# Attention's products with V: two rounded products a key tile replaced by one float32 product, issued in two bursts a head

## The chip, the cores and the metric

The kernel runs on one core of one Trainium2 chip. The metric is the device time of one execution in microseconds; of several executions the median stands. A core has a matrix engine (TensorE, PE in the profile; its weight loads are listed apart as PEld), VectorE (DVE), ScalarE (ACT), GpSimd (POOL) and SyncE (SP), which issues most of the DMAs here. The engines run beside one another and wait for one another through semaphores. Each works off its own queue in order.

## What is computed

One inference step of a hybrid diffusion transformer with two layers: 1024 latent tokens (and 128 cached context tokens that they also read) and 128 tokens of a new prompt, model width 1024. Each layer mixes tokens in three ways side by side, grouped-query attention (GQA: 6 query heads, 2 key/value heads, width 64), latent attention (MLA: 4 heads) and a state-space model, projects the three together, and goes through an MLP. The change touches this part only:

```python
def block_attention(q, k, v, scale):
    ...
        s = jnp.einsum('bqgrd,bsgd->bgrqs', qblk, k).astype(F32) * scale
        pr = jax.nn.softmax(s, axis=-1).astype(v.dtype)
        return jnp.einsum('bgrqs,bsgd->bqgrd', pr, v)
```

All of it is in float32. Latent queries attend to 9 tiles of 128 keys (one of cached context, eight latent); queries of the new prompt attend to one tile, their own.

## The kernel before

**Precision.** Most products are made in the fast rounded type `fp32r`: a float32 operand is split into a rounded part and the rest (`cp`, line 65, casts; `lo`, line 78, subtracts), and the products of the parts are added up in PSUM. `mm` (line 69) issues a product, `tr` (line 73) a transpose against the identity. The modulation (`m<-raw,cT` in the profile) instead multiplies plain float32 tiles: four products of 32 columns of the array each, on quarters of it, side by side.

**Tiling of attention.** `mix` prepares keys and values, builds a list of 30 heads (a `Group` each) and calls `attn`. Queries come in three blocks `b` of 384 columns: blocks 0 and 1 hold latent queries, block 2 has 256 latent queries and 128 of the prompt. So there are 12 MLA heads ("first kind": three products a score tile, with `KT` and `KR`) and then 18 GQA heads ("second kind": two products, with `KY`) a layer. Of the 60 heads of both layers 40 have 384 columns and nine key tiles, 20 have 256 columns for the nine latent key tiles and 128 columns for key tile 9.

**One step.** The loop of `attn` goes over the heads and, in a head, over its key tiles `j`. A step j transposes the probabilities `P` of key tile j+2 into `pt` (PSUM; `trans`, two steps ahead), makes one score tile of the next head (`score`: products into `S`, and VectorE's copy with a running maximum, line 777, into `P`; after three of them ScalarE's exponential), and adds key tile j to the output `oT` (`prod`). `trans` splits the transposed tile: `ph` is ScalarE's cast and `pl` VectorE's subtraction. `prod` makes two products, with `ph` and with `pl`; the weights are `V(j)`, the rounded and the low part of the values side by side, 128 columns. So rows 0 to 63 of `oT` hold the sum with the rounded values and rows 64 to 127 that with the low parts. At the end of a head `fin1` copies `oT`, and `fin2` transposes it back, adds its two halves and scales by the row sums.

**Values.** The MLA values are made in the preamble of `mix` (ten tiles, each a ScalarE cast and a VectorE subtraction into `V`, line 919). The GQA values and keys are loaded in the background by `kv_gqa`, in four steps; the values are split by ScalarE and GpSimd into `VY`.

**Order of the work.** The program is written in the order of the loop, and a scheduler orders every engine's queue by priority, as a simulation of the timeline sees operands become ready. Between steps, `pull` lets background work (a state-space part, the output projection and post-norm of the block before, the modulation) issue a share that a small cost account (`spend`) allows. PSUM has two tiles `S`, three `pt`, one `oT`.

Of the kernel before, what the change touches and what calls it, by code (L numbers as in the profile page):

```python
# [4 lines left out]
F32 = mybir.dt.float32  # L5
R = mybir.dt.float32r
# [10 lines left out]
BK = 384  # L17
# [20 lines left out]
class Net:  # L38
# [711 lines left out]
    def attn(self, groups, tp, ps):  # L750
# [41 lines left out]
        def trans(g, j):  # L792
            rw = rows(g, j)
            c0, c1 = rw[0] * 128, rw[-1] * 128 + 128
            pt = ps.tile([128, BK], F32, name="pt", bufs=3)
            kc = j if j < 9 else 0
            for i in rw:
                self.tr(pt[:, i * 128:i * 128 + 128], g.P[i][:, kc * 128:kc * 128 + 128])
            ph = tp.tile([128, BK], R, name="ph", bufs=3)
            pl = tp.tile([128, BK], R, name="pl", bufs=3)  # L800
            self.cp(ph[:, c0:c1], pt[:, c0:c1])
            self.lo(pl[:, c0:c1], pt[:, c0:c1], ph[:, c0:c1])
            return ph[:, c0:c1], pl[:, c0:c1], c0, c1

        def prod(g, j, t):
            ph, pl, c0, c1 = t
            if j == 0:
                g.oT = ps.tile([128, BK], F32, name="oT", bufs=1)
            first, last = j in (0, 9), j in (8, 9)
            self.mm(g.oT[:, c0:c1], g.V(j), ph, first, False)  # L810
            self.mm(g.oT[:, c0:c1], g.V(j), pl, False, last)

# [23 lines left out]
        for n, g in enumerate(groups):  # L836
            nx = groups[n + 1] if n + 1 < ng else None
            nj = 9 if g.nq == 3 else 10
            ts = [trans(g, 0), trans(g, 1)]
            for j in range(nj):  # L840
                if j + 2 < nj:
                    ts.append(trans(g, j + 2))
                if nx and j < 9:
                    score(nx, j // 3, j % 3)
                prod(g, j, ts[j])
                if j == 1 and prev:
                    fin2(prev)
                if j == 5 and n + 2 < ng:
                    begin(groups[n + 2])
                self.pull(g.pull)  # L850
            fin1(g)
            prev = g
            if g.after:
                g.after()
# [13 lines left out]
    def mix(self, l):  # L868
# [50 lines left out]
        V = xm.tile([128, 10, 4, 2, 64], R, name="V")  # L919
        for j in range(10):  # L920
# [6 lines left out]
            self.cp(V[:, j, :, 0, :], p3)  # L927
            self.lo(V[:, j, :, 1, :], p3, V[:, j, :, 0, :])
# [20 lines left out]
        VY = kv.tile([128, 10, 2, 2, 64], R, name="VY")  # L949
        KY = kv.tile([128, 2, 1280], R, name="KY")  # L950
        self.bg += [self.kv_gqa(l, VY, KY, ss, blk), self.ssm_b(l, ss)]
# [13 lines left out]
        for b in range(NB):  # L965
            for h in range(4):
# [22 lines left out]
                groups.append(Group(b, prep, lambda j, h=h: V[:, j, h].rearrange("p v d -> p (v d)"),  # L989
# [10 lines left out]
        for b in range(NB):  # L1000
            for h in range(6):
# [33 lines left out]
                groups.append(Group(b, prep, lambda j, h=h: VY[:, j, h // 3].rearrange("p v d -> p (v d)"),  # L1035
# [275 lines left out]
    def kv_gqa(self, l, V, KT, tp, blk):  # L1311
        nc, a = self.nc, self.a
        for j0, j1 in ((0, 3), (3, 6), (6, 9), (9, 10)):
            n = j1 - j0
            kt = tp.tile([128, 3, 128], F32, name="zsl", bufs=2)
            vt = tp.tile([128, 3, 128], F32, name="zsl", bufs=2)
            for z, cache, scr in ((kt, "c_k", self.s_qk[:, :, 384:512]), (vt, "c_v", self.s_v)):
                f = 1 if j0 == 0 else 0
                if f:
                    self.dma(z[:, 0], a[cache][l].rearrange("p g d -> p (g d)"))  # L1320
                self.dma(z[:, f:n], scr[j0 + f - 1:j1 - 1].rearrange("t p c -> p t c"))
            yield D[4]
            v4 = vt[:, :n].rearrange("p t (g d) -> p t g d", d=64)
            for g in range(2):
                self.cp(V[:, j0:j1, g, 0, :], v4[:, :, g])
                self.lo(V[:, j0:j1, g, 1, :], v4[:, :, g], V[:, j0:j1, g, 0, :], nc.gpsimd)
# [296 lines left out]
```

## Time and profile before

| | before |
|---|---|
| median of 3 runs (lowest, highest) | 3482.16 us (3480.79, 3486.63) |
| the profiled execution | 3485.52 us |
| its span, first to last instruction | 3483.7 us |
| TensorE busy, share of the span | 3234.2 us, 93% |
| weight loads | 3055.2 us, 88% |
| VectorE | 2257.0 us, 65% |
| ScalarE | 1557.5 us, 45% |
| GpSimd | 1348.8 us, 39% |
| mean granted TensorE clock | 0.963 of full speed |

The table is the first part of the profile page. Busy shares are means over stages with different limits, so they say which engine has most to do, not which one sets the end of a given stage. A product's row gives the time from its start to the end of its drain; products overlap, so the time from one start to the next is shorter than the row's duration. Attention runs from 398 to 886 us in layer 0 and from 2130 to 2592 us in layer 1.

### The profile page before, as it was taken

To read this page: it belongs to the slowest core of one execution; us is meant where nothing else is said; L and a number is where in the kernel's file an instruction comes from. 1 tells how busy PE (TensorE), PEld (TensorE's weight loads), DVE (VectorE), ACT (ScalarE), POOL (GpSimd) and SP (SyncE) were. 2 spreads that over 40 slices of the span, in tenths; PEclk is the share of its full clock that TensorE was granted. 3 is DMA by queue.
4 is the path that set the end of the run, shared out by engine and by line. 5 is a ranking of instruction groups with operands and counts; after the bars stand their busy time and mean duration, and the time that the engine had idled before them with its cause. 6 is when DMAs were issued, how large, how long until landed. Compare 5 with 4: busy or idle time off the path is not lost. (4 is left out here: it accounts for less than half of the span.)

```text
span 3483.7 us, 50649 instructions
## 1 busy us (share of the span) xinstructions
PE 3234.2 (93%) x18578; PEld 3055.2 (88%) x18578; DVE 2257.0 (65%) x5318; ACT 1557.5 (45%) x3250; POOL 1348.8 (39%) x996
## 2 busy tenths in 40 slices
PE   6988799998899999999989887999888999999997
PEld 3966698788799999999989676989887999999997
DVE  6876888765647778774588767887658223333236
ACT  4464677665441221112454646787654411222223
POOL 6357432144651122113573673331356412111145
PEclk8989899999999999999999998999998999999999
DMA  5253333413332333322432533322233211111134
GB/s 212 80 175 104 115 86 116 164 49 97 126 103 80 94 99 98 91 91 73 145 120 97 170 112 111 89 92 67 79 108 98 85 37 45 41 43 43 37 97 145
DMA packets 164525, 340.71 MB, mean 98 GB/s; under 512 B 14429, under 2 KB 105909, under 8 KB 160693
## 3 DMA queue, kind: packets, MB, share of 16 engines
q1 hardware_dynamic: 161012, 335.32, 30.2%
q8 instruction: 146, 2.39, 0.3%
q10 hardware_dynamic: 3264, 2.16, 0.2%
q14 instruction: 103, 0.84, 0.1%
HBM read 280.99 MB, written 56.44 MB: 97 GB/s over the span
## 5 line engine op out<-in xcount | busy, mean ns | idle before, releaser
L78 POOL TENSOR_TENSOR w<-raw,w 128x1024 fp32r<-128x1024 f32 (+1 forms) x266 | 650.6, 2451 | 1370.8 <-ACT w L65 1314.8
L69 PE MATMUL g<-h,w 128*128 128x384 f32 x5328 | 971.5, 342 | 10.5 <-DVE h L78 6.4
L69 PEld LDWEIGHTS g<-h,w 128*128 128x128 f32 x5328 | 949.5, 190 | 16.5 <-DVE h L78 8.6
L69 PE MATMUL g<-big,w 128*128 128x384 f32 x4608 | 818.7, 336 | 8.4 <-DVE big L78 3.4
L69 PEld LDWEIGHTS g<-big,w 128*128 128x128 f32 x4608 | 802.5, 189 | 12.4 <-DVE big L78 5.2
L65 ACT CAST w<-raw 128x1024 fp32r<-128x1024 f32 (+1 forms) x266 | 275.9, 1042 | 643.5 <-PE g L69 353.1
L83 DVE TENSOR_TENSOR big<-big,g 128x384 f32<-128x384 f32 x336 | 181.8, 550 | 289.4 <-PE g L69 289.1
L83 DVE TENSOR_TENSOR r<-r 128x384 f32<-128x384 f32 x192 | 148.5, 773 | 329.0 <-ACT r L97 328.4
L69 PE MATMUL g<-w,h 128*128 128x512 f32 (+1 forms) x1296 | 321.6, 402 | 31.1 <-ACT w L65 12.2
L777 DVE TENSOR_SCALAR_CACHE_REDUCE P<-S 128x384 f32<-128x384 f32 (+1 forms) x500 | 265.8, 541 | 112.3 <-PE S L69 108.3
L69 PEld LDWEIGHTS g<-w,h 128*128 128x128 f32 x1296 | 252.7, 199 | 77.4 <-ACT w L65 13.5
L78 DVE TENSOR_TENSOR pl<-pt,ph 128x384 fp32r<-128x384 f32 (+2 forms) x560 | 267.7, 498 | 43.4 <-ACT ph L65 39.7
L65 ACT CAST ph<-pt 128x384 fp32r<-128x384 f32 (+2 forms) x560 | 232.2, 445 | 84.4 <-PE pt L73 72.1
L93 DVE SCALAR_TENSOR_TENSOR macc<-raw,cT,macc 128x128 f32<-128x128 f32 x784 | 259.9, 393 | 0.0
L73 PE MATMUL pt<-cst,P 128*128 128x128 f32 x1460 | 257.9, 276 | 0.5 <-DVE pl L78 0.3
L97 ACT ACTIVATE r<-g 128x384 f32<-128x384 f32 x192 | 94.2, 491 | 355.2 <-PE g L69 354.9
L78 DVE TENSOR_TENSOR big<-r,big 128x384 fp32r<-128x384 f32 x192 | 172.3, 897 | 92.6 <-ACT big L65 92.4
L69 PE MATMUL op<-big,w 128*128 128x384 f32 x1152 | 227.3, 340 | 2.0 <-DVE big L78 1.6
L97 ACT ACTIVATE P<-P,mx 128x1152 f32<-128x1152 f32 x180 | 210.4, 1170 | 37.0 <-DVE mx L89 36.0
L69 PEld LDWEIGHTS op<-big,w 128*128 128x128 f32 x1152 | 199.2, 188 | 3.2 <-DVE big L78 2.2
L73 PEld LDWEIGHTS pt<-cst,P 128*128 128x128 f32 x1460 | 189.3, 142 | 14.1 <-ACT P L97 0.9
L65 ACT CAST big<-r 128x384 fp32r<-128x384 f32 x192 | 98.4, 513 | 195.8 <-DVE r L83 195.6
(291 smaller groups left out, 4782.9 us busy)
## 6 DMA issues: line engine op xcount, KB each, us to landing
raw<-in_w SPq DMA_DIRECT2D x176, 512.0 KB, 3.5
raw<-in_w_mod SPq DMA_DIRECT2D x80, 512.0 KB, 3.7
raw<-in_w_out SPq DMA_DIRECT2D x48, 512.0 KB, 3.7
big<-s_x SPq DMA_DIRECT2D x13, 1536.0 KB
E<-s_ac SPq DMA_DIRECT2D x36, 384.0 KB, 4.4
s_x<-big SPq DMA_DIRECT2D x9, 1536.0 KB, 5.1
cv<-s_cv SPq DMA_DIRECT2D x36, 320.0 KB, 3.9
h<-in_w_mod SPq DMA_DIRECT2D x16, 512.0 KB, 9.9
```

The lines of the kernel that those rows point to most:

```text
L65: self.nc.scalar.copy(out, in_)
L69: self.nc.tensor.matmul(out, lhsT=lhsT, rhs=rhs, start=start, stop=stop)
L73: self.nc.tensor.transpose(out, in_, self.ident[:p, :p])
L78: (eng or self.nc.vector).tensor_tensor(out=out, in0=src, in1=hi.bitcast(F32), op=ALU.subtract)
L83: (eng or self.nc.vector).tensor_tensor(out=out, in0=a, in1=b, op=op)
L93: self.nc.vector.scalar_tensor_tensor(out=out, in0=a, scalar=s, in1=b, op0=op0, op1=op1)
L97: self.nc.scalar.activation(out=out, in_=in_, func=func, **kw)
L777: nc.vector.tensor_scalar(out=p[:, j * 384:j * 384 + nk], in0=S, scalar1=1.0, scalar2=None, op0=ALU.mult, op1=ALU.max, accum_out=mx[:, j:j ...
```

## The change

Each transposed tile is no longer split. It is copied once to float32 (`pT`, eight buffers instead of three `ph` and three `pl`), by VectorE for j = 1, 4, 7 and by ScalarE for the others. The values stay float32, 64 columns, and a key tile takes one float32 product instead of two rounded ones. Even key tiles go to rows 0 to 63 of `oT`, odd ones to rows 64 to 127, so two products use one half of the array's columns each; `fin2` adds the halves as before. Key tile 8, which has no partner, is cut into two halves of its query columns, one on each side; key tile 9 takes all 128 columns, with values whose second half is zero (`V9`, `VY9`).

The products of a head are issued in two bursts: key tiles 3, 2, 1, 0 at j = 3, and the rest (8, 7, 6, 5, 4, and 9) at the last step. The burst is raised in priority by 120, and its instructions are stamped with an order token that tells the scheduler to keep them together. The cost account charges other sums. The MLA values are copied once in the preamble, with no subtraction. The GQA values are loaded by three DMAs where the pools of attention are opened, straight into their place, and `kv_gqa` handles keys alone.

```diff
         def trans(g, j):
...
-            ph = tp.tile([128, BK], R, name="ph", bufs=3)
-            pl = tp.tile([128, BK], R, name="pl", bufs=3)
-            self.cp(ph[:, c0:c1], pt[:, c0:c1])
-            self.lo(pl[:, c0:c1], pt[:, c0:c1], ph[:, c0:c1])
-            return ph[:, c0:c1], pl[:, c0:c1], c0, c1
-
-        def prod(g, j, t):
-            ph, pl, c0, c1 = t
-            if j == 0:
+            pT = tp.tile([128, BK], F32, name="pT", bufs=8)
+            if j % 3 == 1:
+                self.spend(2, pt[:, c0:c1], 1.04, 68)
+                nc.vector.tensor_copy(pT[:, c0:c1], pt[:, c0:c1])
+            else:
+                self.cp(pT[:, c0:c1], pt[:, c0:c1])
+            return pT[:, c0:c1], c0, c1
+
+        def prods(g, js, ts):
+            if js[0] == 0:
                 g.oT = ps.tile([128, BK], F32, name="oT", bufs=1)
-            first, last = j in (0, 9), j in (8, 9)
-            self.mm(g.oT[:, c0:c1], g.V(j), ph, first, False)
-            self.mm(g.oT[:, c0:c1], g.V(j), pl, False, last)
+            with self.tc.high_priority(120):
+                for j in sorted(js, key=lambda j: (j == 9, -j)):
+                    pT, c0, c1 = ts[j]
+                    self.spend(0, pT, 0.9, 0)
+                    if j == 8:
+                        cm = (c0 + c1) // 2
+                        parts = [(0, c0, cm), (64, cm, c1)]
+                    else:
+                        parts = [(64 * (j % 2), c0, c1)]
+                    for r0, a0, a1 in parts:
+                        r = slice(0, 128) if j == 9 else slice(r0, r0 + 64)
+                        i = nc.tensor.matmul(g.oT[r, a0:a1], lhsT=g.V(j), rhs=pT[:, a0 - c0:a1 - c0],
+                                             start=j in (2, 3, 9), stop=j in (4, 5, 9))
+                        self.tc.stamp_issue_order_token(i.ins, "pv")
...
                 if nx and j < 9:
                     score(nx, j // 3, j % 3)
-                prod(g, j, ts[j])
+                if j == 3:
+                    prods(g, range(4), ts)
+                if j == nj - 1:
+                    prods(g, range(4, nj), ts)
                 if j == 1 and prev:
...
-        V = xm.tile([128, 10, 4, 2, 64], R, name="V")
+        V = xm.tile([128, 9, 4, 64], F32, name="V")
+        V9 = xm.tile([128, 4, 2, 64], F32, name="V9")
+        nc.gpsimd.memset(V9[:, :, 1], 0.0)
...
-            self.cp(V[:, j, :, 0, :], p3)
-            self.lo(V[:, j, :, 1, :], p3, V[:, j, :, 0, :])
+            self.cp(V[:, j] if j < 9 else V9[:, :, 0], p3)
...
-        VY = kv.tile([128, 10, 2, 2, 64], R, name="VY")
+        VY = kv.tile([128, 9, 2, 64], F32, name="VY")
+        VY9 = kv.tile([128, 2, 2, 64], F32, name="VY9")
+        nc.gpsimd.memset(VY9[:, :, 1], 0.0)
+        self.dma(VY[:, 0], a["c_v"][l])
+        self.dma(VY[:, 1:9].rearrange("p t g d -> p t (g d)"), self.s_v[0:8].rearrange("t p c -> p t c"))
+        self.dma(VY9[:, :, 0], self.s_v[8].rearrange("p (g d) -> p g d", g=2))
         KY = kv.tile([128, 2, 1280], R, name="KY")
-        self.bg += [self.kv_gqa(l, VY, KY, ss, blk), self.ssm_b(l, ss)]
+        self.bg += [self.kv_gqa(l, KY, ss, blk), self.ssm_b(l, ss)]
...
-            v4 = vt[:, :n].rearrange("p t (g d) -> p t g d", d=64)
             for g in range(2):
-                self.cp(V[:, j0:j1, g, 0, :], v4[:, :, g])
-                self.lo(V[:, j0:j1, g, 1, :], v4[:, :, g], V[:, j0:j1, g, 0, :], nc.gpsimd)
```

## Rows read from the trace of the kernel before

**Rows 1.** Windows of attention, two layers; columns: stretch, us, busy (xinstructions), PEclk, DMA, GB/s

```profile
398.00:886.00 488.00, 461.81 (x2999) 415.79 (x3000) 360.67 (x1179) 338.40 (x746) 171.47 (x150) 0.97 0.33 104
2130.00:2592.00 462.00, 433.95 (x2838) 403.06 (x2838) 355.40 (x1163) 333.26 (x737) 169.93 (x150) 0.97 0.27 83
```

**Rows 2.** Timeline of PE, ordinary steps; columns: start, duration, engine, operation, shapes, count

```profile
586.25 0.33 PE L69 MATMUL S<-KY,qh 128*128 128x384 f32 x1
...
586.59 0.34 PE L69 MATMUL oT<-pl,VY 128*128 128x384 f32 x1
586.77 0.49 PE L73 MATMUL pt<-cst,P 128*128 128x128 f32 x3
587.01 0.42 PE L69 MATMUL S<-KY,qh 128*128 128x384 f32 x1
587.27 0.33 PE L69 MATMUL S<-KY,ql 128*128 128x384 f32 x1
```

**Rows 3.** Timeline of PE, products of a head with 256 columns

```profile
847.58 0.28 PE L69 MATMUL oT<-ph,VY 128*128 128x256 f32 x1
847.70 0.28 PE L69 MATMUL oT<-pl,VY 128*128 128x256 f32 x1
```

**Rows 4.** Window over heads of the second kind in a row, layer 1; columns as rows 1

```profile
2340.00:2380.00 40.00, 39.77 (x270) 37.00 (x269) 38.63 (x141) 35.38 (x75) 2.03 (x4) 1.00 0.06 16
```

**Rows 5.** Groups by line and form: the split; busy us, mean ns, idle before and releaser

```profile
L78 DVE TENSOR_TENSOR pl<-pt,ph 128x384 fp32r<-128x384 f32 x360 | 192.0, 550 | 20.0 <-ACT ph L65 17.7
L78 DVE TENSOR_TENSOR pl<-pt,ph 128x256 fp32r<-128x256 f32 x180 | 70.5, 418 | 16.5 <-ACT ph L65 15.1
L65 ACT CAST ph<-pt 128x384 fp32r<-128x384 f32 x360 | 163.8, 488 | 60.4 <-PE pt L73 55.0 <-DVE pl L78 2.6 <-PE oT L69 1.0
L65 ACT CAST ph<-pt 128x256 fp32r<-128x256 f32 x180 | 63.8, 379 | 21.3 <-PE pt L73 14.5 <-PE oT L69 1.9 <-DVE P L777 1.8
```

**Rows 6.** Group by line and form: the float32 products of the modulation inside attention

```profile
L69 PE MATMUL m<-raw,cT 128*32 128x512 f32 x96 | 18.8, 602 | 1.2 <-DMA raw<-in_w_mod 1.2
```

**Rows 7.** Timeline of PE around float32 products on quarters of the columns

```profile
581.33 0.34 PE L69 MATMUL S<-KY,ql 128*128 128x384 f32 x1
581.60 1.90 PE L69 MATMUL m<-raw,cT 128*32 128x512 f32 x10
583.43 0.44 PE L69 MATMUL oT<-ph,VY 128*128 128x384 f32 x1
583.80 1.04 PE L69 MATMUL m<-raw,cT 128*32 128x512 f32 x2
584.77 0.45 PE L69 MATMUL oT<-pl,VY 128*128 128x384 f32 x1
585.06 0.49 PE L73 MATMUL pt<-cst,P 128*128 128x128 f32 x3
```

**Rows 8.** Timeline of PE's weight loads, the same stretch

```profile
581.59 0.16 PEld L69 LDWEIGHTS m<-raw,cT 128*32 128x32 f32 x8 [0.26 <-DVE mx L782]
```

**Rows 9.** Waits of PEld, layer 0, then layer 1; us in total, times, longest

```profile
PEld S L69 <- DVE P L777: 20.0, 17, 6.1
PEld S L69 <- DVE pl L78: 3.3, 6, 0.8
...
PEld S L69 <- DVE P L777: 21.4, 17, 6.1
PEld oT L69 <- DVE pl L78: 5.7, 18, 1.1
```

**Rows 10.** Timeline of DVE and PE at a post-norm; idle before, releaser in brackets

```profile
750.34 7.30 DVE L89 TENSOR_SCALAR big<-big,der 128x384 f32<-128x384 f32 x6
...
758.17 0.69 PE L69 MATMUL S<-KY,qh 128*128 128x384 f32 x1 [5.14 <-DVE P L777]
```

**Rows 11.** Chain of work that ended last, layer 1's preamble: start, us

```profile
2126.38 3.45 DVE V L78 x10
```

**Rows 12.** DMA issues: queue, operation, count, KB each, us from issue to landing

```profile
raw<-in_w SPq DMA_DIRECT2D x176, 512.0 KB, 3.5
```

More of the change, by code (lines that the diff above doesn't have):

```diff
@@ L987, in done @@
                         self.dma(self.s_o[3 * b:3 * b + 3, :, 0:256].rearrange("t p c -> p t c"), blk["ob"])
-                groups.append(Group(b, prep, lambda j, h=h: V[:, j, h].rearrange("p v d -> p (v d)"),
+                groups.append(Group(b, prep, lambda j, h=h: V[:, j, h] if j < 9 else V9[:, h].rearrange("p v d -> p (v d)"),
                                     96.0 ** -0.5, dst, done, PU[3]))
@@ L1033, in done @@
                     blk["oo"] = oh, ol
-                groups.append(Group(b, prep, lambda j, h=h: VY[:, j, h // 3].rearrange("p v d -> p (v d)"),
+                groups.append(Group(b, prep, lambda j, h=h: VY[:, j, h // 3] if j < 9 else VY9[:, h // 3].rearrange("p v d -> p (v d)"),
                                     0.125, dst, done, PU[4]))
@@ L1309, in ssm_b, with kv_gqa @@
             yield from second(t)
-    def kv_gqa(self, l, V, KT, tp, blk):
+    def kv_gqa(self, l, KT, tp, blk):
         nc, a = self.nc, self.a
@@ L1315, in kv_gqa @@
             kt = tp.tile([128, 3, 128], F32, name="zsl", bufs=2)
[L1316 to L1321, printed above, removed]
+            f = 1 if j0 == 0 else 0
+            if f:
+                self.dma(kt[:, 0], a["c_k"][l].rearrange("p g d -> p (g d)"))
+            self.dma(kt[:, f:n], self.s_qk[j0 + f - 1:j1 - 1, :, 384:512].rearrange("t p c -> p t c"))
             yield D[4]
-            v4 = vt[:, :n].rearrange("p t (g d) -> p t g d", d=64)
             for g in range(2):
-                self.cp(V[:, j0:j1, g, 0, :], v4[:, :, g])
-                self.lo(V[:, j0:j1, g, 1, :], v4[:, :, g], V[:, j0:j1, g, 0, :], nc.gpsimd)
                 kd = tp.tile([128, 3, 2, 64], F32, name="xt", bufs=2)
```

## The prediction

> **What bounds the kernel now.** I read the page's first part, then the two attention stretches by windows, then single groups and the order in time of the instructions that the change replaces. TensorE is the busiest engine of the page. Attention (layer 0 from 398 to 886 us, layer 1 from 2130 to 2592 us) is the only place that the change touches, so it is read from there [rows 1]: of 950 us TensorE is busy 895.8, VectorE 716.1, ScalarE 671.7. A busy TensorE there includes the drain of each product, so the reader should rather count steps from start to start. Three products of 384 columns in a row (the middle one is left out of the rows) fill the time from 586.25 to the transposes at 586.77 [rows 2]: 0.173 us each, though a row says 0.33. Three transposes and one product take 0.50 us (586.77 to 587.27), so a transpose takes 0.109. Products of 256 columns step by 0.12 [rows 3].
>
> By these steps a head of the second kind without work beside it (18 score products, 27 transposes, 18 products with V, 6 small transposes) costs TensorE 6.2 + 3.6 = 9.8 us. Where such heads follow one another, VectorE is busy 38.6 of 40 us and TensorE 39.8 [rows 4]; its 270 instructions there are 3.9 heads of 69, so a head takes 10.2. So attention is balanced: TensorE is the bound and VectorE is hardly behind it. That makes the sign depend on two small differences: what the new products cost TensorE, and how much of TensorE's waiting came from the step that goes.
>
> **The change, part by part.**
>
> *Removed splits.* The 560 subtractions that make `pl` go: 360 of 550 ns, 180 of 418 ns and 20 small ones, 262.5 us of VectorE's time in the two main forms [rows 5]. Three of nine copies come back to VectorE (j = 1, 4, 7). No plain copy of this shape from PSUM stands in the trace; the nearest row is `pl` itself, which reads the same PSUM tile, so I take its 550 and 418 ns: a third of 262.5, 88 us. VectorE is relieved of 175 us, ScalarE of the third that moved, (163.8 + 63.8)/3 = 76 us [rows 5]. Neither is on the path as such, since TensorE was the bound; they count only through waits.
>
> *Removed and added products.* Whether two float32 products run side by side on one half of the columns each can be read, since the modulation of layer 0 does it with quarters (32 columns) between the heads. The code asks for 48 products there and 96 stand in the trace, so one float32 product is two passes, "halves" below [rows 6]. One product alone (two halves) occupies TensorE from 583.80 to the next start at 584.77, 0.97 us; ten halves, four products side by side and one alone behind, from 581.60 to 583.43, 1.83 us [rows 7]. The four thus cost 0.86, two rounds of 0.43, and the lone one two rounds and 0.11 for filling and draining. A round of 512 columns is 0.43, of 384 by columns 0.32, of 256 0.215. Going in costs 0.27 instead of 0.173 (581.33 to 581.60), 0.10; the product behind the tiles steps by 0.29 (584.77 to 585.06) instead of 0.173, 0.12. With the 0.11 a burst costs 0.32 over its rounds.
>
> A head with 384 columns: four products in the first burst are 4 rounds, five in the second are 5 (key tile 8 is cut in two halves of the columns), 9 x 0.32 + 2 x 0.32 = 3.52 us, against 18 x 0.173 = 3.11: 0.41 more, 40 heads, 16 us. A head with 256 columns: 9 x 0.215 + 0.64 = 2.58, and key tile 9 as one full-width float32 product of 128 columns, by the round two passes of 0.11 and their weights, 0.2 to 0.4, taken at 0.3: 2.88 against 18 x 0.12 + 0.2 = 2.36: 0.52 more, 20 heads, 10 us. **TensorE gets 27 us more to do**, nothing covers it where TensorE is the bound. Bounds: 20 (a burst that enters from a gap hides its entry) to 40 (a scheduler that now and then lets something into a burst).
>
> *The Trainium skill, weighed.* In the trace the eight weight loads of the four tiles stand within 0.16 us, all ahead of the second round, and the halves run four at a time [rows 7, 8]. The Trainium skill ("TensorE: Matmul & The Clock Gate", section "Part 3: Packing small matmuls — row/col tiling") states that a weight load overlaps products in flight only when the row groups differ, and that products keep program order in start and end. By that rule, with both tiles over all rows here, a burst would come out longer; the trace does not agree, and the rival below prices it.
>
> *New waits.* TensorE's queue now holds a burst until the copy of its last tile is there (j = 3 and j = 8, both ScalarE copies). Behind it are transposes and scores, for which ScalarE's copies and VectorE's score copies wait. The trace has no such wait; the nearest are the waits on `pl` that go, 5.7 us in layer 1 over 18 times, 0.3 each [rows 9]. The burst asks only for copies made two steps earlier, so I take 0.04 at each of 120 bursts, 5 us, with 0 and 0.2 each (24 us) as bounds. The eight `pT` buffers replace three and three, so transposes are held back later than now.
>
> *Waits that go.* (1) TensorE's weight loads waiting on `pl`: 3.3 for scores in layer 0 and 5.7 for V products in layer 1 are the two rows of rows 9; with the smaller rows of the same kind some 12 us. (2) Scores waiting on VectorE's copy of the scores: 20.0 and 21.4 us [rows 9]. About 22 of these are four waits of 5 to 6 us, like the one at 758.17, where VectorE is in six scalings of the post-norm that take 7.30 us [rows 10]; those scalings stay where they are. Of the other 19 I take 11, as VectorE has a quarter less to do (175 of 716). (3) In the four heads around these scalings VectorE is the bound: six subtractions less are 6 x 0.55 = 3.3 us in a head of 384 columns and 2.5 in one of 256; two of each, 10 us after rounding down. (4) Waits shorter than a drain, which no row shows as idle: 5 us, an estimate from the 40 us of rows 4, where 10.2 us a head stand against 9.8 of steps. Sum 38 us.
>
> *Moves at one price.* The V splits of the preamble (10 on VectorE, 3.45 us on the chain in layer 1 [rows 11]) go, but ScalarE still makes the ten copies in the same stretch and KR's copies queue behind them: taken at 0, bounds -7 to 0 over the layers. The GQA values now come by three loads at the start of the psx stage instead of eight in steps; they sit on SP's queue ahead of the first loads of the background (keys, M, cv). They are needed only at the first head of the second kind, some 165 us later, so 0; without that cover a load of this size would cost what a 512 KB weight load takes to land, 3.5 us a layer [rows 12]. The sixteen casts and sixteen subtractions on ScalarE and GpSimd for them go, and the two memsets are small: 0.
>
> **The sum.** +27 +5 -38 = -6 us against the profiled execution of 3485.5 us (span 3483.7 and 1.8 around it), which is 3.4 above the median of the three runs, 3482.2. On the median: **3476 us**, 0.18% less.
>
> **The rivals.**
> *VectorE was the bound all along* (faster). For it: 38.6 of 40 us in rows 4. Then nearly all visible idle time of TensorE in rows 1 (488.0 - 461.8 + 462.0 - 434.0 = 54 us) except some 12 at the starts and on loads goes, and some 20 that drains hide (both estimates): -62 + 27 + 5 = -30, **3452 us**. Against it: the four long waits are the scalings'.
> *The bursts starve the path* (slower). While a burst holds TensorE 1.6 to 1.9 us, only two score tiles and three transposed tiles are there for the other engines, and each burst begins by waiting for a ScalarE copy. If a burst start waits 0.2 us (24 us) and the shared waits of (1), (2) and (4) return as waits on scores, only a little of the 38 comes back, 25: 27 + 24 - 25 = +26, **3508 us**. It decides from (38 - 27)/120 = 0.09 us of wait per burst.
> *The halves do not pair as in the modulation* (slower). With products in strict program order each burst takes one round more, 80 x 0.32 + 40 x 0.215 = 34 us: 3510. If they do not overlap at all, another 9 rounds a head, 40 x 2.88 + 20 x 1.94 = 154 us: 3630. That is also the case in which the change does not do what it says. Rows 7 and 8 speak against both.
>
> **How the numbers follow.** The forecast holds 0.45, the faster rival 0.25, the starving bursts 0.23, the pairing rival 0.07. The forecast's own range, 3464 to 3488, comes from the bounds of the burst and of the waits; 0.2% (7 us) is about what a measurement of this kernel can tell from no change, so faster begins below 3475.2, and of the 0.45 I give 0.20 to faster, 0.20 to no change and 0.05 to slower. Faster: 0.20 + 0.25 = 0.45; same 0.20; slower 0.05 + 0.23 + 0.07 = 0.35. The range takes in both near rivals with some room for their own bounds, 3446 to 3518, and leaves out the unpaired case.
>
> **What would show it.** Right: V products at 0.32 us from round to round, two at a time; 120 bursts, each of 8 to 10 halves (plus two for key tile 9) with nothing of TensorE between them; heads without work beside them at 10.2 to 10.4 us as before (10.2); VectorE at some 27 instead of 38 of 40 us there; TensorE's waits on `pl` gone and the four long waits still there. Wrong: a V product that waits on its `pT` for more than 0.1 us as a rule (third rival), single halves alone in the array (pairing), or pure heads below 9.8 us (my step for a burst is too dear).

## The result, and the profile after

The changed kernel takes **3518.39 us** (median of 4 runs, 3515.53 to 3518.99); the kernel before, on the same chip, 3481.47. The ratio is 1.0103 with a 95% interval of 1.0086 to 1.0121: 1% slower, where 0.18% faster was forecast. The time lies 0.4 us above the range. The profiled execution took 3518.60 us, and the rows below are from it. First the head of its page: span, and busy time by engine.

```profile
span 3516.8 us, 49806 instructions
...
PE 3251.3 (92%) x18698; PEld 2957.4 (84%) x18698; DVE 2109.0 (60%) x4918; ACT 1491.4 (42%) x3054; POOL 1345.1 (38%) x984
```

TensorE has 17 us more to do than before, VectorE 148 less, and the span is 33.1 us longer: the relief of VectorE did not pay for the rest. The windows that answer to [rows 1, 4] (stretch, length, busy time and count of each engine, granted clock, DMA share, GB/s; the last is six heads of the second kind in a row):

```profile
398.50:893.00 494.50, 467.58 (x3053) 364.37 (x3054) 284.38 (x989) 305.09 (x650) 167.41 (x144) 0.97 0.31 98
2146.30:2622.00 475.70, 444.07 (x2890) 353.88 (x2889) 286.73 (x973) 300.75 (x639) 165.49 (x143) 0.96 0.25 76
2348.90:2412.80 63.90, 63.22 (x431) 45.73 (x431) 44.48 (x171) 47.09 (x97) 3.05 (x6) 1.00 0.07 21
```

Heads in a row take 10.65 us each, where the prediction's sign of being right was 10.2 to 10.4; VectorE is busy 28 of 40 us there, as predicted (27).

The loss is in three places. I cut each layer at four marks: its first score product, the first and the last copy of `oT` (the bodies of attention lie between these), and the 201st product `g<-big,w` of the MLP, from where both kernels run in step. Both layers together, us against the kernel before; "rest" is everything else, the preambles among it. Each row is one profile, and executions of one kernel differ (17 of the kernel before took 3477.8 to 3491.0 us), so a single difference of a few us proves little:

| | first heads | bodies | tails | rest | span |
|---|---|---|---|---|---|
| before (length) | 48.0 | 877.3 | 310.3 | 2248.1 | 3483.7 |
| changed kernel | +9.0 | +12.5 | +13.8 | -2.2 | +33.1 |
| e1 relief | +0.9 | -13.9 | +6.7 | -0.4 | -6.8 |
| e2 rounded bursts | -1.5 | -6.7 | +2.7 | -3.8 | -9.3 |
| e3 tiles elsewhere | +10.7 | +10.3 | +5.1 | +1.6 | +27.7 |
| e4 free order | +9.0 | +2.9 | +18.7 | -7.8 | +22.7 |
| e5 values in steps | +14.3 | +13.5 | +1.5 | -8.4 | +20.9 |
| e6 one burst | +9.4 | +22.2 | +3.6 | -1.6 | +33.7 |
| e7 pairs | +13.3 | +67.8 | +11.2 | -0.1 | +92.3 |
| e8 ScalarE copies | +15.9 | +10.5 | +5.0 | -5.9 | +25.5 |
| e9 subtractions back | +3.6 | +9.9 | +4.8 | -1.3 | +16.9 |
| e10 side effects off | +6.8 | -2.2 | +4.0 | -6.7 | +1.9 |
| e11 before, few products | +1.2 | -57.7 | -2.1 | -3.3 | -61.8 |
| e12 changed, few products | +9.3 | -99.5 | +14.2 | -4.7 | -80.8 |

The prediction spoke of the bodies alone. Their windows, before and then after:

```profile
421.64:873.56 451.92, 428.96 (x2808) 386.43 (x2806) 338.42 (x1106) 316.00 (x699) 147.15 (x122) 0.97 0.31 100
2157.79:2583.22 425.43, 404.42 (x2664) 376.15 (x2661) 330.91 (x1086) 311.01 (x687) 147.35 (x122) 0.98 0.25 76
```

```profile
426.15:879.38 453.23, 433.49 (x2867) 335.29 (x2866) 263.39 (x919) 285.07 (x611) 144.40 (x121) 0.98 0.31 99
2174.56:2611.13 436.57, 413.29 (x2720) 328.73 (x2720) 262.73 (x896) 280.79 (x597) 144.77 (x121) 0.97 0.24 74
```

TensorE is busy 13.4 us more (833.4 to 846.8) and idle for 44.0 us before, 43.0 after (length less busy). VectorE works 143 us less there, and TensorE waits as long as it did.

**The burst** looks as predicted. Timeline of TensorE in a head of 384 columns (start, duration, shapes, count):

```profile
2374.63 0.49 PE L73 MATMUL pt<-cst,P 128*128 128x128 f32 x3
2375.05 1.51 PE L825 MATMUL oT<-pT,VY 128*64 128x384 f32 x8
2376.49 0.87 PE L73 MATMUL pt<-cst,P 128*128 128x128 f32 x6
2377.12 0.42 PE L69 MATMUL S<-KY,qh 128*128 128x384 f32 x1
```

and of its weight loads (idle time before them in brackets, with its reason; "issue" is none that the profile shows):

```profile
2375.04 0.20 PEld L825 LDWEIGHTS oT<-pT,VY 128*64 128x64 f32 x4 [0.17 <-issue]
2375.42 0.14 PEld L825 LDWEIGHTS oT<-pT,VY 128*64 128x64 f32 x2 [0.18 <-issue]
2375.74 0.14 PEld L825 LDWEIGHTS oT<-pT,VY 128*64 128x64 f32 x2 [0.18 <-issue]
2376.49 0.64 PEld L73 LDWEIGHTS pt<-cst,P 128*128 128x128 f32 x6 [0.60 <-issue]
```

Four products, eight halves, take 1.44 us to the next transpose; a round is 0.32 (2375.42 to 2375.74), so four are 1.28 and 0.16 comes on top; the three transposes ahead take 0.42 instead of 3 x 0.109, and the six behind take 0.63 to the start of the next product, where [rows 2] (0.24 for three, 0.109 for each more) would have 0.57: some 0.3 us in all. The transposes' weights come only when the burst is over. In the kernel before they were loaded while the product ahead (from 586.59 to 586.93 in [rows 2]) was still running:

```profile
586.60 0.42 PEld L73 LDWEIGHTS pt<-cst,P 128*128 128x128 f32 x3
```

The Trainium skill ("TensorE: Matmul & The Clock Gate", section "Part 3: Packing small matmuls — row/col tiling") says that a weight load overlaps products in flight only where the row groups differ. The 0.60 us behind the burst agrees with that rule; the row at 586.60 does not, and neither do the four loads within 0.20 us at the start of the burst, two of them for the second round while the first runs: all of these use all 128 rows. So the rule does not explain the wait. The rows of waits add up such waits (weight loads; us in total, times, longest; the layer 0 window above, then two lines of layer 1):

```profile
PEld pt L73 <- issue: 28.4, 52, 1.2
...
PEld S L69 <- DVE P L777: 19.0, 17, 5.6
...
PEld oT L825 <- ACT pT L65: 2.2, 8, 0.5
...
PEld S L69 <- DVE P L777: 24.5, 25, 5.7
...
PEld oT L825 <- ACT pT L65: 2.8, 12, 0.4
```

The 28.4 us are no loss by themselves, since TensorE is busy with the bursts meanwhile. Against [rows 9]: the waits on `pl` are gone, but those on VectorE's score copies are not (20.0 and 21.4 before, 19.0 and 24.5 now).

### The profile page after: what moved, and what is told of

The parts are those of the page before. It is cut to its first block, busy times and chain, and to the rows that moved or that the text cites. A ratio compares the mean times of both kernels' runs of the same rounds, so it can differ in the third digit from the quotient of the medians.

```text
span 3516.8 us, 49806 instructions
## 1 busy us (share of the span) xinstructions
PE 3251.3 (92%) x18698; PEld 2957.4 (84%) x18698; DVE 2109.0 (60%) x4918; ACT 1491.4 (42%) x3054; POOL 1345.1 (38%) x984
## 5 line engine op out<-in xcount | busy, mean ns | idle before, releaser
L73 PE MATMUL pt<-cst,P 128*128 128x128 f32 x1460 | 240.8, 280 | 5.6 <-DVE pT L802 3.3
L73 PEld LDWEIGHTS pt<-cst,P 128*128 128x128 f32 x1460 | 173.0, 141 | 81.7 <-issue 56.7
L65 ACT COPY pT<-pt 128x384 f32<-128x384 f32 (+2 forms) x380 | 156.8, 439 | 102.8 <-PE pt L73 100.7
L83 POOL TENSOR_TENSOR big<-big 128x768 f32<-128x768 f32 x72 | 134.5, 1887 | 42.7 <-DVE big L83 17.5
```

Of the source, the lines that this page charges most:

```text
L65: self.nc.scalar.copy(out, in_)
L73: self.nc.tensor.transpose(out, in_, self.ident[:p, :p])
L83: (eng or self.nc.vector).tensor_tensor(out=out, in0=a, in1=b, op=op)
```

## The experiments

The theories that they were to tell apart: (A) float32 products have a price of their own, at entry and drain of every burst; (B) bursts starve the other engines, which then keep TensorE waiting; (C) the relief of VectorE was never worth what the prediction took; (D) the first heads and tails are side effects of what else was moved.

**e1: the relief alone.**

```diff
-            pl = tp.tile([128, BK], R, name="pl", bufs=3)
-            self.cp(ph[:, c0:c1], pt[:, c0:c1])
-            self.lo(pl[:, c0:c1], pt[:, c0:c1], ph[:, c0:c1])
-            return ph[:, c0:c1], pl[:, c0:c1], c0, c1
+            if j % 3 == 1:
+                nc.vector.tensor_copy(ph[:, c0:c1], pt[:, c0:c1])
+            else:
+                self.cp(ph[:, c0:c1], pt[:, c0:c1])
+            return ph[:, c0:c1], ph[:, c0:c1], c0, c1
```

> The kernel before, with the subtractions left out and three of nine copies of a transposed tile moved to VectorE; both products of a key tile then use the same rounded tile, so the low part is left out of the result. TensorE's instructions are those of before; only VectorE and ScalarE are relieved, as in the change. Predicted step (the waits that go): about -38 us, 3444. If the relief was worth only what the attention bodies of the changed kernel show (its TensorE waits fell by 23 us): 3459. If VectorE's work never mattered: 3482. If VectorE was the bound all along: 3425 or less.

Measured: 3475.83 us, ratio 0.9965 [0.9952, 0.9978], 12 us less by the ratio. The 23 us of the expectation are not in the windows of the bodies, where the idle time of TensorE in the changed kernel had fallen by 1.0. Bodies of e1 (windows), and its largest waits of weight loads on VectorE's score copies, layer 0 and layer 1:

```profile
418.97:860.28 441.31, 424.80 (x2805) 383.50 (x2803) 270.86 (x923) 286.54 (x611) 144.44 (x121) 0.98 0.32 102
2151.90:2573.94 422.04, 404.24 (x2661) 375.10 (x2659) 268.97 (x903) 281.74 (x599) 144.95 (x121) 0.98 0.26 80
```

```profile
PEld S L69 <- DVE P L777: 19.2, 23, 4.1
...
PEld S L69 <- DVE P L777: 19.9, 32, 3.5
```

VectorE has 129 us less to do in the bodies (669.3 to 539.8), TensorE the same products; it idles 34.3 us instead of 44.0. The bodies shrink by 13.9 us where the prediction had 38. The waits on score copies, of which it wanted 11 back, gave 2.3. Heads of the second kind in a row show it best, four before, then five in e1:

```profile
2339.30:2380.60 41.30, 41.08 (x278) 38.13 (x278) 39.94 (x147) 36.08 (x77) 2.03 (x4) 1.00 0.06 16
```

```profile
2334.10:2385.70 51.60, 51.40 (x354) 47.68 (x352) 38.90 (x148) 40.18 (x82) 2.54 (x5) 1.00 0.07 19
```

VectorE falls from 97% to 75% of the time, and a head takes 10.3 us in both.

**e2: the bursts with rounded products.** On top of e1:

```diff
-            ph = tp.tile([128, BK], R, name="ph", bufs=3)
+            ph = kv.tile([128, BK], R, name="ph", bufs=8)
...
-                prod(g, j, ts[j])
+                if j == 3:
+                    prods(g, range(4), ts)
+                if j == nj - 1:
+                    prods(g, range(4, nj), ts)
```

(`prods` issues both rounded products of each key tile, in the changed kernel's order, priority and token; `kv` is the pool of the GQA keys and values.)

> The kernel of the run before this one (no subtractions, the low part left out), with its rounded products issued in the two bursts of the changed kernel, from eight buffers. Against that kernel, the starving theory (a burst leaves the other engines without work and TensorE then waits for score copies) expects 15 to 30 us more; the theory that the price is that of float32 products (entry, drain, weight loads held back) expects no more than 5 us more.

Measured: 3483.04 us, ratio 0.9997 [0.9974, 1.0020]; against e1 some 11 us by the ratios (its ten runs spread from 3474 to 3516), 7.2 in the bodies (863.4 to 870.6 us, one profile each):

```profile
418.48:867.59 449.11, 426.24 (x2813) 384.85 (x2810) 267.14 (x924) 285.97 (x615) 144.81 (x122) 0.98 0.31 100
2150.99:2572.45 421.46, 397.25 (x2666) 374.15 (x2664) 265.39 (x902) 279.41 (x600) 145.15 (x121) 0.98 0.25 77
```

Between the two expectations. TensorE idles 47.1 us, 13 more than in e1. But e2 has the raised priority and the token too, so this is the price of bursts with both, and e4 and e10 below give back more than 7.2 us for these two alone: that bursts as such starve is not shown by it.

**e3: the tiles elsewhere.** The changed kernel with

```diff
-            pT = tp.tile([128, BK], F32, name="pT", bufs=8)
+            pT = kv.tile([128, BK], F32, name="pT", bufs=8)
...
-        self.attn(groups, at, ps)
+        self.attn(groups, at, ps, kv)
```

> The changed kernel with its eight buffers for the transposed tiles taken from the memory pool of the GQA keys and values instead of attention's own pool; instructions are the same. Theory of the tail: the 3 KB by which attention's own pool grew make the MLP's first two loads reuse memory that comes free later, so they queue behind a weight load on SyncE, and the stretches behind attention, 7.9 and 5.9 us longer than before, come back: 3518 - 14 = 3505. If the tails are longer because background work was left over from attention: 3518.

Measured: 3513.58 us, ratio 1.0074 [1.0057, 1.0091]; the interval touches the changed kernel's. Of the 13.8 us of the tails 8.7 went, 7.5 of them in layer 0. SyncE's queue there, in the changed kernel and then in e3 (start, us to issue, the transfer):

```profile
901.08 0.33 SPq L54 DMA_DIRECT2D raw<-in_w  x1
901.46 0.91 SPq L54 DMA_DIRECT2D big<-s_x  x2
```

```profile
878.26 0.33 SPq L54 DMA_DIRECT2D big<-s_x  x1
...
898.03 0.32 SPq L54 DMA_DIRECT2D big<-s_x  x1
900.37 2.91 SPq L54 DMA_DIRECT2D raw<-in_w  x2
```

`big<-s_x` are the first two loads of the MLP's norm. In the changed kernel both stand behind a weight load, and TensorE later waits for what is made of them; in e3 the first goes out before attention ends. Nothing but the pool of `pT` differs: eight buffers instead of three and three made attention's own pool 3 KB larger, and the scheduler then gave the loads a later place. The rest of the tails (5.1 us) did not come back, and the place of these loads is not all: e1, with no larger pool, has +6.7, and e7 and e12 send the first load before attention ends, as e3 does, and still have +11.2 and +14.2.

e3 differs from e2 by float32 instead of rounded products, and by the values' loads and splits. Its bodies are 17.0 us longer (870.6 to 887.6), TensorE is busy 20.4 us more:

```profile
426.33:878.67 452.34, 432.09 (x2855) 333.74 (x2853) 262.57 (x911) 283.31 (x608) 144.14 (x121) 0.98 0.31 99
2168.98:2604.24 435.26, 411.85 (x2723) 328.33 (x2722) 263.35 (x899) 280.85 (x600) 144.80 (x121) 0.97 0.24 74
```

**e4: free order.** The changed kernel with

```diff
-            with self.tc.high_priority(120):
...
-                        self.tc.stamp_issue_order_token(i.ins, "pv")
```

> The changed kernel without the raised priority and without the order token: the scheduler may place each float32 product where it likes. If keeping the bursts whole is what costs, several us faster, 3505 to 3512; if it breaks bursts up, each further break costs a product's entry and drain, 0.3 us: 3520 to 3535; if the two bursts come out whole by themselves, since all but one of their tiles are long ready, no difference: 3518 within 3.

Measured: 3508.59 us, ratio 1.0059 [1.0044, 1.0074]. Most bursts come out whole by themselves (125 of four and more halves, 123 with the token), yet the bodies are 9.6 us shorter than the changed kernel's, at the same work of TensorE (845.8 us busy, 34.3 idle instead of 43.0). So it isn't that they are whole which costs, but the raised priority and the token (where they put the bursts, or what they hold back); the two were not tried apart. The tails, 4.9 us longer, take half of it back; this run has `pT` in its old pool.

**e5: the values in steps.** On top of e3, the three loads go, and `kv_gqa` again loads values and keys by turns (`vt` beside `kt`) and has ScalarE copy them:

```diff
-        self.dma(VY[:, 0], a["c_v"][l])
...
+                self.cp(V[:, j0:j1, g] if j0 < 9 else V9[:, g:g + 1, 0], v4[:, :, g])
```

> The changed kernel with its buffers moved as in the run on the memory pool, and the GQA values again loaded by the background in four steps, two steps' copies to float32 by ScalarE ahead of each step's keys, as before (no subtraction). Theory of the first head: with the values gone from that background, the keys' casts and subtractions fall into the first head, TensorE idles between its first score tiles and works at the lower clock; the two first heads, 6.8 and 3.8 us longer than before, come back: 3514 - 10 = 3504. If the first heads are longer for another reason (the missing subtractions of the MLA values, the buffers): 3514.

Measured: 3506.56 us, ratio 1.0061 [1.0041, 1.0081], but not where it was expected: the first heads did not come back (+14.3 against +10.7). The theory fell.

**e9: the subtractions back.** What else the first heads of e1 and e2 have and the changed kernel hasn't are the subtractions of the MLA values. Timeline of VectorE at the first head of the changed kernel, then windows of its second, third and fourth 4 us after the first score, and the third and fourth in the kernel before:

```profile
399.46 0.55 DVE L777 TENSOR_SCALAR_CACHE_REDUCE P<-S 128x384 f32<-128x384 f32 x1
...
403.35 0.56 DVE L78 TENSOR_TENSOR KY<-m,KY 64x384 fp32r<-64x384 f32 x1 [3.32 <-ACT KY L65]
403.94 0.56 DVE L777 TENSOR_SCALAR_CACHE_REDUCE P<-S 128x384 f32<-128x384 f32 x1
```

```profile
400.20:404.20 4.00, 2.48 (x11) 1.91 (x10) 0.82 (x2) 1.92 (x4) 2.09 (x3) 0.71 1.03 349
404.20:408.20 4.00, 2.44 (x10) 1.91 (x10) 2.78 (x10) 3.03 (x6) 4.00 (x6) 0.72 0.57 175
408.20:412.20 4.00, 4.00 (x17) 3.81 (x16) 2.42 (x9) 1.85 (x5) 0.69 (x1) 0.50 0.35 111
```

```profile
406.00:410.00 4.00, 3.77 (x23) 3.27 (x24) 3.45 (x14) 3.82 (x8) 4.00 (x5) 1.00 0.53 157
410.00:414.00 4.00, 3.82 (x26) 3.31 (x24) 3.88 (x16) 3.56 (x9) 0.91 (x3) 1.00 0.42 131
```

VectorE stands 3.32 us on a key subtraction whose cast is not there, with the score copies queued behind it. TensorE, with two score tiles, runs dry (2.48 and 2.44 of 4 us busy), and then makes the next products at a granted clock of 0.50, the lower level of 1.2 GHz, where before has 1.00. On top of e3:

```diff
+            vd = xb.tile([128, 4, 64], F32, name="vd", bufs=2)
+            self.tt(vd, p3, V[:, j] if j < 9 else V9[:, :, 0], ALU.subtract)
```

> The changed kernel with moved buffers, and in each layer's preamble ten subtractions put back on VectorE, of the size of those that split the MLA values before (their result isn't used). They do nothing but take 3.5 us of VectorE between the last key tile and the first score. Revised theory of the first head: without them the first score starts some 2 to 3.5 us earlier, while the background's loads come no earlier; the keys' casts and subtractions then stand in VectorE's queue ahead of the first score copies, TensorE idles and makes the first head's products at the lower clock. Then the added work makes the kernel faster, the two first heads fall from 30.5 and 28.3 us to 24 and 25, the preamble takes 2 us more in layer 0: 3514 - 7 = 3507. If the first heads are slow for the bursts' sake, the added work costs its time: 3514 to 3520.

Measured: 3502.88 us, ratio 1.0057 [1.0037, 1.0076] (e3: 1.0074; the intervals overlap, so the trace decides). The first heads take 26.9 and 24.8 us instead of 30.5 and 28.3, the first score of layer 0 comes 3.1 us later, the span is 10.7 shorter. Added work of no use makes the first heads 7.1 us shorter, of e3's 10.7: theory (D) holds for that part. The second 4 us after the first score in e9:

```profile
402.90:406.90 4.00, 2.05 (x11) 1.23 (x11) 2.77 (x9) 2.88 (x7) 3.51 (x4) 1.00 0.62 186
```

TensorE runs dry here too, but for one such stretch and not three (the first 4 us of the changed kernel have 2.48 busy as well), and the clock stays up behind it. VectorE's wait for the key's cast is still 2.23 us (3.68 in e3, 0.58 before), so the cause is eased and not gone. In e10 the same subtractions leave the first heads at 28.1 and 26.8, 2.2 us less than in e4: how much they give back depends on the rest of the order, and why is open.

**e10: side effects off.** The edits of e4, e3 and e9 together (no priority, no token, `pT` from `kv`, `vd`).

> The changed kernel without raised priority and token, with moved buffers and with the ten subtractions of the run before this one. If the accounting by stretches is complete, what is left of the change is the bodies of attention alone, as the run in free order has them (-4.9 and +7.8 us), with tails and first heads as before: 3 us over the kernel before, 3488 where that is 3485, between 3481 and 3495. If the tails and first heads were chance of one schedule and others take their place: 3500 or more. If the price of the bursts lies in the stretches outside: below 3478.

Measured: 3489.42 us (12 runs), ratio 1.0015 [1.0004, 1.0026]: 5 us more than before by the ratio. Its bodies:

```profile
421.86:866.47 444.61, 429.07 (x2855) 334.11 (x2853) 263.88 (x911) 284.21 (x608) 144.50 (x121) 0.98 0.31 101
2152.28:2582.76 430.48, 411.33 (x2711) 326.92 (x2709) 261.95 (x891) 279.76 (x595) 144.36 (x121) 0.98 0.24 75
```

The sum is what the accounting had, but its parts are not, so that is partly luck: the bodies are at -2.2 instead of +2.9, the first heads at +6.8 and the tails at +4.0 instead of 0, and the rest at -6.7. What it does show comes from e9, from which it differs by the priority and the token alone: 13.5 us less in time, 12.1 of it in the bodies, as e4 had 9.6. It is the best of the changed kernels and does not beat the one before.

**e6 and e7: fewer and more bursts.** On top of e3, first all products at the last step, from eleven buffers, key tile 8 whole on one side:

```diff
-                if j == 3:
-                    prods(g, range(4), ts)
                 if j == nj - 1:
-                    prods(g, range(4, nj), ts)
+                    prods(g, range(nj), ts)
```

and then, from eight buffers again, in pairs:

```diff
-                if j == 3:
-                    prods(g, range(4), ts)
-                if j == nj - 1:
-                    prods(g, range(4, nj), ts)
+                if j % 2 and j < 8:
+                    prods(g, range(j - 1, j + 1), ts)
+                if j == nj - 1:
+                    prods(g, range(8, nj), ts)
```

> The changed kernel with moved buffers, eleven of them, and all products with V of a head in one burst at its last step (key tile 8 whole on one side, half a round more, 0.16 us a head). If a burst has a price of its own (entry, drain, first transposes held back: about 0.3 us), 60 bursts fewer save 18 us less 10: 3506. If bursts starve the other engines, one of 3.3 us starves them more than two of 1.4 and 1.8: 3525 to 3545. If neither: 3523.

> The changed kernel with moved buffers and its products with V issued in pairs of key tiles, as soon as both are there: five bursts a head instead of two. If a burst has a price of its own of about 0.3 us, 180 more cost 54: 3568. If starving is what costs, shorter bursts give it back: 3495 to 3505.

Measured: e6 3519.27 us, ratio 1.0096 [1.0071, 1.0122]; e7 3574.57 us, 1.0255 [1.0226, 1.0284]. The bodies of e7:

```profile
428.24:911.98 483.74, 466.27 (x2862) 329.11 (x2862) 267.94 (x916) 286.26 (x608) 143.12 (x121) 0.98 0.29 93
2209.43:2670.79 461.36, 442.80 (x2721) 320.82 (x2719) 269.28 (x899) 282.74 (x600) 143.81 (x121) 0.98 0.22 70
```

e7 makes 328 unbroken runs of products with V instead of e3's 141 and its bodies are 57.5 us longer, 0.31 us for each more: theory (A), to the size that was predicted (TensorE is busy 65.1 us more and idle 7.6 less, so shorter bursts give back little). e6, with 64 runs fewer, should by that price be some 8 us shorter and its bodies are 11.9 longer. Transposes wait for copies on VectorE there (13.1 us in layer 0, one wait of 6.9, against 4.6 in e3), as (B) would have it; but TensorE's idle time grows by 2.4 us alone and its busy time by 9.5, which is the half round. Waits shorter than a drain do not show as idle time, so where the saved entries went is not shown. The price of 0.3 us is shown for breaking bursts up, not for joining them.

**e8: all copies on ScalarE.** On top of e3:

```diff
-            if j % 3 == 1:
+            if False:
```

> The changed kernel with moved buffers and all nine copies of the transposed tiles on ScalarE: VectorE is relieved of another 180 copies of about half a microsecond, ScalarE gets them. If VectorE's score copies are what TensorE waits for, as the predicted gain had it, 5 to 12 us faster: 3502 to 3509. If ScalarE's copies then come late for the bursts: 3520 to 3530. If neither is on the path: 3514.

Measured: 3509.15 us, ratio 1.0070 [1.0047, 1.0094], the bodies +10.5 against e3's +10.3. VectorE is busy 458 us there instead of 526, and nothing moves: a second relief of VectorE is worth nothing here. ScalarE took the copies, so a small gain and a small loss could cancel.

**e11 and e12: what the products with V cost in all.** In the kernel before, and in e3, only key tiles 8 and 9 are multiplied:

```diff
-                prod(g, j, ts[j])
+                if j >= 8:
+                    prod(g, j, ts[j])
```

```diff
-                if j == 3:
-                    prods(g, range(4), ts)
                 if j == nj - 1:
-                    prods(g, range(4, nj), ts)
+                    prods(g, range(8, nj), ts)
```

> The kernel before with the products with V of key tiles 0 to 7 left out; transposes, casts and subtractions stay. By the steps of the prediction 16 products of 0.173 us go in each of 40 heads and 16 of 0.12 in 20 heads: 149 us of TensorE. If TensorE is the bound all through attention, all of it comes off: 3336. If VectorE is hardly behind it, as the rows of heads in a row say (38.6 of 40 us busy), these heads cannot fall below 9.6 us, and half or less comes off: 3400 to 3440.

> The changed kernel with moved buffers and the products with V of key tiles 0 to 7 left out (key tile 8 is then multiplied whole on both halves of the columns, one round a head); the copies stay. By the predicted cost of a burst 60 bursts of four products go and 60 shrink to one round: about 2.9 us in each of 40 heads and 2.0 in 20: 156 us, from 3514 to 3358 if all comes off. If TensorE's waits, rather than its work, had become the bound, well less: 3400 or more. The difference to the run before it tells what the relief of VectorE is worth once TensorE's share is gone.

Measured: e11 3424.70 us, ratio 0.9840 [0.9809, 0.9871]; e12 3398.13 us, 0.9764 [0.9709, 0.9818]. Bodies of e11, then of e12:

```profile
417.49:836.35 418.86, 378.51 (x2341) 315.64 (x2340) 328.68 (x1106) 310.92 (x699) 145.52 (x122) 0.95 0.34 108
2121.37:2522.13 400.76, 361.56 (x2196) 303.91 (x2196) 323.36 (x1086) 306.01 (x687) 146.22 (x123) 0.96 0.26 81
```

```profile
420.81:821.34 400.53, 369.69 (x2393) 306.67 (x2394) 261.02 (x913) 281.53 (x607) 142.69 (x120) 0.97 0.35 112
2118.24:2495.51 377.27, 351.73 (x2249) 298.03 (x2249) 261.96 (x893) 275.44 (x598) 143.39 (x120) 0.97 0.27 85
```

e11 lies in the range that balanced engines were to give, e12 beside the 3400 that was to mean that waits had become the bound. Of 149 us of products (an estimate from the steps of the prediction) the kernel before gets back 57.7 in the bodies, 0.39 for each microsecond taken from TensorE. Of 156 (an estimate likewise) the changed kernel gets back 109.8 (887.6 to 777.8), 0.70. And from e11 to e12 the bodies fall by 41.8 us (819.6 to 777.8), where the relief of VectorE with all products in place gave 13.9 (e1). So the two engines were balanced before: taking work from either gives back a part, because the other comes up behind it. Once VectorE is relieved most of TensorE's work counts.

## Why the prediction was wrong, point by point

- **TensorE's added work** (27 us, bounds 20 to 40): right in kind, too large. A round takes 0.32 us, halves run two at a time, a burst costs 0.3 us over its rounds (0.32 predicted; 0.31 by e7). From e2 to e3 the bodies grew by 17.0 us, under the bounds, and TensorE's busy time by 20.4. Rival three (halves do not pair) is out.
- **New waits** (5 us): TensorE's loads waited 2.2 + 2.8 us for ScalarE's copies, 20 times. Right. Rival two named this wait as the start of the starving, and it is not. What the term left out is how the order is forced: raised priority and token have no price in the prediction, and taking them away shortens the bodies by 9.6 us (e4) and 12.1 (e10 against e9). The 7.2 us from e1 to e2 contain them.
- **Waits that go** (38 us): the step that failed. The relief alone gives 13.9 us in the bodies (e1). Item 2 took 11 of the waits on score copies, and 2.3 went; item 3 took 10 in the heads around the scalings, and the two heads of each layer there went from 31.5 and 32.4 us to 29.6 and 31.8, 2.5 us, while the two heads of 256 columns gave nothing (33.8 before in each layer, 33.9 and 33.6 in e1). Item 4 took 5 us from heads in a row, and these take 10.3 us in both kernels. The waits on `pl` went (item 1), and transposes now wait for the exponential (7.8 us in e1, not among the large rows before). The mistake is one of kind: I took waits off a row by the engine named in it, as if TensorE had nothing else late. That other waits took their place is argued from these rows; that the relief is worth 13.9 us and not 38 is shown.
- **The sum in the bodies**: predicted +27 +5 -38 = -6. By the chain of runs it is -13.9 (e1), +7.2 (e2), +17.0 (e3), +2.2 (the changed kernel): +12.5. Of the 39 us between the forecast and the two profiles (-6 and +33.1), this chain puts 24 on the waits that go and 20.6 on the stretches outside; TensorE's work takes 10 off, and 4 are the bursts and the last step of the chain. Without priority and token the bodies are at +2.9 (e4) and -2.2 (e10), not far from -6, but by two errors against each other: the relief was put 24 us too high, and products and bursts together, 32 in the prediction, cost 11.7 in e10.
- **Moves at one price** (0, bounds -7 to 0): wrong sign. The rest, the preambles among it, gave 2 us and the first heads cost 9.0. The ten subtractions did go from the chain [rows 11], and what they had covered came out: the background's key work at the first score. e9 gives back 7.1 of e3's 10.7, e10 only 2.2 of e4's 9.0, and the rest is open; e5 shows that the loads moved ahead on SyncE are not the cause.
- **The tails** (+13.8 us): not in the prediction at all. It looked for queues that a moved step passes, and not at memory: 3 KB more in one pool changed when two loads of the next stage went out. e3 shows 8.7 us of it. Why the other 5.1 stay is open, and so is why e7 and e12 have more with the loads in their old place.
- **Rival one** (VectorE was the bound all along, 3452): out by e1, which relieves VectorE (and ScalarE by 76 us) with TensorE's products as they were and gains 12 us. Rival two came nearest in time (3508), but that is luck: what it describes is at most 7 of the 33 us.

## What to carry to other kernels

Where two engines are balanced, price a change by what one engine's work costs when the other's is as it is: leaving work out on each side (e1 for VectorE's, e11 for TensorE's) takes two runs and would have said that relief is worth 13.9 of 129 us and that products issued singly cost 0.39 of their time. Going between full-width rounded products and float32 products on half the columns had a price here of 0.3 us each time (what the type and what the half columns have in it was not tried apart), so pairs were too short; from two groups a head to one nothing was gained. Raising the priority of a group and forcing its order is a change of its own, here some 10 us, and wants a run without it. After a change of buffers, look at the loads of the stage behind it: their place in the queue can move.

## What was not expected of the hardware

- The weights of the transposes behind a float32 burst on half the columns are loaded only when it has ended: 0.60 us without a weight load in the rows shown, 28.4 us over 52 such waits in layer 0. Behind a full-width rounded product they are loaded while it runs.
- Ten subtractions of no use, 3.45 us of VectorE, made the two first heads 7.1 us shorter. Without them, in layer 0 of the changed kernel, TensorE ran dry (2.48 and 2.44 of 4 us busy) and made the products of the next 4 us at a granted clock of 0.50; with them, in e9, the clock behind the dry stretch (2.05 of 4) stayed at 1.00. In layer 1 the granted clock of the first 16 us averages 0.79 in e3 and 0.81 in e9 (windows of 4 us), so the 3.5 us that came back there are not the clock's.
